# Depthwise-convolution taps all on VectorE at low scheduling priority, and the triangular inverse's masked copies as one VectorE operation

## The chip, the cores and the metric

One core of one Trainium2 chip. The metric is the device time of one execution of the whole program, in microseconds (us). Five engines run side by side, each through its own queue in order: TensorE (PE in the profile; its weight loads are PEld), VectorE (DVE), ScalarE (ACT), GpSimd (POOL) and SyncE (SP), which here issues the DMA transfers.

## The reference

Two blocks in a row over 512 tokens of width 1024. The first is a mixer with attention and a convolution branch, the second a linear-attention recurrence (RWKV-7 style) with a feed-forward part behind it. What matters here:

```python
def conformer_conv(glu_in, conv_w, conv_b, ln_w, ln_b, w_pw, b_pw):
    a, g = jnp.split(glu_in, 2, axis=-1)
    u = a * jax.nn.sigmoid(g)                       # 512 channels
    y = depthwise_conv(u, conv_w, width=31, centred) + conv_b
    y = jax.nn.silu(layer_norm(y, ln_w, ln_b))      # over channels
    return y @ w_pw + b_pw

# block 1
p = u @ w_in[l]                     # q, k, v, attention gate, GLU inputs, conv gate
attn = attend_blocked(q, k_all, v_all) * silu(p[..., ZA])
conv = conformer_conv(p[..., GLU], ...) * silu(p[..., ZC])
h = h + gate * (concatenate([attn, conv], -1) @ w_out[l])

# block 2, for every head, over 512 steps
def step(S, inp):
    r_t, w_t, k_t, v_t, a_t, b_t = inp
    sa = einsum('bhvk,bhk->bhv', S, a_t)
    S = S * w_t + outer(sa, b_t) + outer(v_t, k_t)
    return S, einsum('bhvk,bhk->bhv', S, r_t)
# then the feed-forward part: x + relu(rms_norm(x) @ w_ff1)**2 @ w_ff2
```

## The kernel before

Activations lie with features on the 128 partitions and the 512 tokens along the free side, so a tile is 128x512. Every fp32 projection is made of three reduced-precision matmuls: `split` (L140) makes a high part of a weight or an activation on ScalarE and the low part (what is left over) by a subtraction on VectorE, and `mm3` (L181) multiplies high by high, high by low and low by high. `Weights` (L160) streams 512 KB weight tiles in the order of use: DMA into `wr`, high part `wh` on ScalarE, low part `wl` on VectorE, with two `wr`, three `wh` and two `wl` buffers. One such weight tile feeds 24 matmuls of 512 columns. So `wl<-wr,wh` on VectorE stands ahead of every projection.

A scheduler orders the instructions of each engine when the program is built, by dependencies, by priorities (which follow the order of the code) and by its own picture of how long things take. From then on each engine works through its list in order and waits at whichever entry isn't ready.

Block 1 (`block1`, L345) runs in these stages:

- the modulation vectors and the first projections, up to about 84 us. They give three of the four GLU tiles (`glu`, L467; 128 channels each); the fourth comes of the projection pair `pa`, `pg`.
- then the q projection (four weight tiles), the context's norm (`modw` tiles) and the k/v projection (two weight tiles), eight gate projections (`zgate`, L595), the rotary embedding (`rope_q`, `rope_k`), a Newton iteration for the norms' square roots on VectorE (`newton`, L230, tiles `nr`), and the key tiles `kst`.
- attention: four head pairs by two halves. `scores` (L755) makes a 128x768 score tile `s` on TensorE, its maximum by a VectorE TENSOR_REDUCE, and the exponential on ScalarE; `values` (L775) transposes the result on TensorE, copies it on ScalarE (`xb`) and multiplies by the values into `pv`. There are 32 score tiles, and two buffers `s`.
- `ln_pw` (L697), a generator that the attention loop steps at the points of `LN_AFTER`: the LayerNorm over the convolution's result (a matmul with ones for the mean, four subtractions, four squares, a matmul for the variance, a square root, a broadcast by transposes, then scale, tanh and product), and the pointwise projection.
- the output projection (`xa` tiles), from about 344 us.

The convolution has 31 taps for each of four tiles `ys[i]` (tile name `hg`). The centre tap makes the tile; each of the other 30 adds a shifted copy of the input times one weight per channel. Before, these 120 are shared out by hand. `conv_pool` (L487) has ScalarE make the product (`cv`) and GpSimd add it, for tiles 0 and 1, 60 taps; `tick` paces it by the TensorE matmuls. `conv_self` (L511) does both on GpSimd, for 15 taps of tile 3. `conv_vec` (L521) does a tap as one VectorE scalar_tensor_tensor in place, 45 taps. The tables PACE, CVZ, CVQ, CONV and CSELF say how many go where.

Block 2 (`block2`, L1292) has six head pairs `p` by two halves `gi`, thus 12 passes of `gen_abc` (L945). A pass builds a unit lower-triangular system out of 64-token chunks and inverts it by block doubling in fp16: the 8x8 diagonal blocks first (`Dm`, `DT`, `P1`, `D2`, ...), then three levels of merging, where a level uses `OT[j]`, the system masked to the blocks of that level. `Lh` is the fp16 system and `k.m16` holds four fp16 masks. All these are 128x512 fp16 tiles named `f`. At the end, `IX` is identity minus the inverse, for one correction step. `OT` (three products a pass) and `IX` (one) run on GpSimd. So do the small Newton iterations of `prep` and `finish` (tiles `nr`, 128x8), which stay there. Projections for the next pairs fill TensorE in between. From 817 us on comes the feed-forward part.

Of the kernel before, what the change touches and what calls it, by code (L numbers as in the profile page):

```python
# [22 lines left out]
P = 128  # L23
# [136 lines left out]
class Weights:  # L160
# [172 lines left out]

LN_AFTER = (4, 4.5, 5, 5.5, 6.5, 7, 7.5, 7.5, 7.5, 8)
MODW = 10
PACE = 6
CVZ = (2, 1, 2, 0, 3, 4, 3, 3)
CVQ = (8, 9, 9, 8)
CTX = (0, 2)
CONV = (0, 0, 0, 0, 0, 0, 0, 0)  # L340
CSELF = (30, 0, 0, 1, 0, 1, 0, 0)
WARM = (8, 20, 0)
ZG = (1, 0, 1, 1, 1, 0, 0, 0, 0, 0, 0)

def block1(k, I, st, h1d):  # L345
# [130 lines left out]
    todo = [[w for w in range(31) if w != 15] for _ in range(4)]

    def tap(i):
        w = todo[i].pop(0)
        o0, o1 = max(0, 15 - w), min(S, S + 15 - w)  # L480
        return o0, o1, up[i][:, o0 + w - 15:o1 + w - 15], k.cw[:, i * 31 + w:i * 31 + w + 1]

    def conv_init(i):
        y = ys[i] = k.t("hg")
        A.activation(y, up[i], AF.Identity, scale=k.cw[:, i * 31 + 15:i * 31 + 16], bias=k.vec("conv_b", i))

    def conv_pool():  # L487
        r = yield
        for i in (0, 1):
            conv_init(i)  # L490
            while todo[i]:
                o0, o1, u, w = tap(i)
                p = k.t("cv")
                t = A.activation(p[:, o0:o1], u, AF.Copy, scale=w)
                if r is not None:
                    k.after(t, r)
                G.tensor_tensor(out=ys[i][:, o0:o1], in0=ys[i][:, o0:o1], in1=p[:, o0:o1], op=ALU.add)
                r = yield
        while True:
            yield  # L500

    cp = conv_pool()
    pace = [0]

    def tick(r, n=1):
        pace[0] += n
        while pace[0] >= PACE:
            pace[0] -= PACE
            cp.send(r)

    def conv_self(i, n):  # L511
        if ys[i] is None:
            y = ys[i] = k.t("hg")
            G.tensor_scalar(out=y, in0=up[i], scalar1=k.cw[:, i * 31 + 15:i * 31 + 16], scalar2=k.vec("conv_b", i), op0=ALU.mult, op1=ALU.add)
        for _ in range(min(n, len(todo[i]))):
            o0, o1, u, w = tap(i)
            p = k.t("cv")
            G.tensor_scalar(out=p[:, o0:o1], in0=u, scalar1=w, scalar2=None, op0=ALU.mult)
            G.tensor_tensor(out=ys[i][:, o0:o1], in0=ys[i][:, o0:o1], in1=p[:, o0:o1], op=ALU.add)

    def conv_vec(i, n):  # L521
        if ys[i] is None:
            conv_init(i)
        for _ in range(min(n, len(todo[i]))):
            o0, o1, u, w = tap(i)
            V.scalar_tensor_tensor(out=ys[i][:, o0:o1], in0=u, scalar=w, in1=ys[i][:, o0:o1], op0=ALU.mult, op1=ALU.add)

    def conv_drain():
        while todo[0] or todo[1]:
            cp.send(None)  # L530
        conv_vec(3, 31)
        assert not any(todo)

    W1 = Weights(k, [I["w_in"][0], I["w_in"][1]] + [I["w_q"][g] for g in range(4)] + [I["w_kv"][g] for g in range(2)]
                 + [I["w_in"][i] for i in (6, 7, 8, 9, 2, 3, 4, 5)] + [I["w_pw"][i] for i in range(2)] + [I["w_out"][i] for i in range(8)])
# [4 lines left out]
        mod_gate(g, mods[g])  # L540
    setup1(k, I)
    k.rest()
    next(cp)
    pa, pg = k.t("pj"), k.t("pv")
    proj(k, pa, W1.next(), us, tick=tick)
    proj(k, pg, W1.next(), us, tick=tick)
    glu(pa, pg)

    q_ps = [k.t("s", [2, S]), k.t("s", [2, S])]
    for g in range(4):  # L550
        wh, wl = W1.next()
        for kk in range(2):
            j = 2 * g + kk
            c = slice(kk * S, (kk + 1) * S)
            for t in range(4):
                tt = slice(t * P, (t + 1) * P)
                uh, ul = us[j]
                ps = q_ps[t // 2][:, t % 2, :]
                T.matmul(ps, uh[:, tt], wh[:, c], start=j == 0, stop=False)
                T.matmul(ps, uh[:, tt], wl[:, c], start=False, stop=False)  # L560
                tick(T.matmul(ps, ul[:, tt], wh[:, c], start=False, stop=j == KT - 1), 3)
        conv_vec(2, CVQ[g])
        if g == CTX[0]:
# [14 lines left out]
    for t in (2, 3, 4, 5, 0, 1):  # L578
        ps = k.t("pt", [256])
        for j in range(KT):  # L580
            wh, wl = kw[j // 4]
            c = slice((j % 4) * 256, (j % 4 + 1) * 256)
            uh, ul = cus[j] if t < 2 else us[j]
            o = (t if t < 2 else t - 2) * P
            tt = slice(o, o + P)
            T.matmul(ps, uh[:, tt], wh[:, c], start=j == 0, stop=False)
            T.matmul(ps, uh[:, tt], wl[:, c], start=False, stop=False)
            tick(T.matmul(ps, ul[:, tt], wh[:, c], start=False, stop=j == KT - 1), 1.5)
        kv = k.t("kvs", [256])
        A.activation(kv, ps, AF.Copy)  # L590
        kvs[t] = kv
# [2 lines left out]
    k.open(st, "zy", dict(kst=2))  # L594
    def zgate(tag):  # L595
        ps = k.t(tag)
        proj(k, ps, W1.next(), us, tick=tick)
        t = k.t("tA")
        A.activation(t, ps, AF.Tanh, scale=0.5)
        g = k.t("hg")  # L600
        V.scalar_tensor_tensor(out=g, in0=t, scalar=1.0, in1=ps, op0=ALU.add, op1=ALU.mult)
        return g
# [58 lines left out]
    def zgates(n):  # L661
        for _ in range(min(n, 8 - len(gz))):
            i = len(gz)
            gz.append(zgate(zt[i] if i < 4 else "pj"))
            conv_vec(3, CVZ[i])

    for i in range(4):
        rope_q(i)
# [139 lines left out]
    for pr in range(4):  # L808
        for half in range(2):
            i = 2 * pr + half  # L810
            pts = scores(pr, half, qs)
            zgates(ZG[3 + i])
            if i == int(LN_AFTER[0]):
                conv_drain()
            for _ in range(LN_AFTER.count(i)):
                next(ln, None)
            conv_vec(3, CONV[i])
            conv_self(3, CSELF[i])
            if half == 1 and pr < 3:
                qs = heads(pr + 1)  # L820
            if len(gz) == 8:
                while done:
                    att_split(done.pop(0))
            if pend is not None:
                if pend[1] == 0:
                    pv = k.t("pv")
                values(*pend, pv)
                if pend[1] == 1:
                    att_out(pend[0], pv)
                    done.append(pend[0])  # L830
            for _ in range(LN_AFTER.count(i + 0.5)):
                next(ln, None)
            pend = (pr, half, pts)
# [111 lines left out]
def gen_abc(k, p, pd, gi):  # L945
# [72 lines left out]
    units(ps, Dm, DT, True, True)  # L1018
    D2T = ev(ps)
    yield  # L1020
    OT = []
    for j in range(1, 4):
        o = k.t("f", [4, P], F16)
        G.tensor_tensor(out=o, in0=Lh, in1=mk(j), op=ALU.mult)
        OT.append(o)
    ps = k.t("i")
    units(ps, D2, D2T, True, True)
    D4T = ev(ps)
# [16 lines left out]
    tok(1)  # L1045
    for j in range(3):
        ps = k.t("i")
        units(ps, OT[j], X, True, True)
        Y = k.t("f", [4, P], F16)
        V.tensor_tensor(out=flat(Y), in0=ps, in1=flat(k.id16x4), op=ALU.add)  # L1050
        yield
        ps = k.t("i")
        units(ps, XT, Y, True, True)
        ps2 = k.t("i")
        units(ps2, Y, XT, True, True)
        X, XT = ev(ps), ev(ps2)
        if j == 0:
            b = k.t("i")
            for u in range(4):
                mm(b[:, u * 64:(u + 1) * 64], MT[:, u, :], Vs[:, u % 2, (u // 2) * 64:(u // 2) * 64 + 64], start=True, stop=True)  # L1060
            A.activation(R4[:, :, 64:128], b[:, 0:256].rearrange("p (u d) -> p u d", u=4), AF.Copy)
        yield
    ps = k.t("i")
    IX = k.t("f", [4, P], F16)
    G.tensor_tensor(out=IX, in0=k.id16x4, in1=X, op=ALU.subtract)
    for u in range(4):
        mm(ps[:, u * P:(u + 1) * P], Lh[:, u, :], X[:, u, :], start=True, stop=False)
        mm(ps[:, u * P:(u + 1) * P], Ll[:, u, :], X[:, u, :], start=False, stop=True)
# [223 lines left out]
def block2(k, I, nm, h1d, out):  # L1292
    A, V, T, G, Y = k.A, k.V, k.T, k.G, k.Y
    P2 = ExitStack()
    k.open(P2, "p2b", dict(lw=1, wa=1, r1=1, AR=2, BK=2, vs=2, UX=2, MT=1, E=3, R4=2, Vs=2, UV=3, W=2, QG=2, sb=2, st=2, f=18))
    k.open(P2, "p2s", dict(s=1), PSUM)
    k.open(P2, "p2i", dict(i=3), PSUM)
    k.open(P2, "p2y", dict(y=1), PSUM)
# [325 lines left out]
```

## Time and profile before

| | us |
|---|---|
| median of 3 runs (1193.18 to 1193.87) | 1193.24 |
| the profiled execution | 1195.04 |
| its span, first to last instruction | 1193.2 |
| PE busy in the span | 1096.6 (92%) |
| DVE busy | 750.1 (63%) |
| ACT busy | 573.7 (48%) |
| POOL busy | 266.3 (22%) |

The profiled execution lies 1.84 us over its own span and the median 0.04 us over that span, so that a change of the span can be taken off the median as it is. The shares are averages over stages of different kinds: PE is busy throughout the last third and far from it between 98 and 226 us, while DVE is the reverse.

### The profile page before, as it was taken

The numbers are of one execution on the slowest core, as the hardware profiler recorded it, in microseconds if no ns is written. First come the engines' busy times: TensorE is split into PE (matmuls) and PEld (weight loads), VectorE is DVE, ScalarE is ACT, GpSimd is POOL, SyncE is SP. The second block draws the span as 40 slices with busy tenths as digits, with TensorE's granted clock in tenths as the row PEclk, the third lists the DMA queues.
The fourth block names the chain that finished last, engine by engine and source line by source line (L and its number), as shares of the span: only waits on it lengthen the run. The fifth ranks groups of instructions, "written<-read, shape, count | busy, mean of one in ns | idle before, by whom it ended". The sixth has DMA issues, their size and how long they took to land.

```text
span 1193.2 us, 16090 instructions
## 1 busy us (share of the span) xinstructions
PE 1096.6 (92%) x6268; PEld 842.1 (71%) x6268; DVE 750.1 (63%) x1161; ACT 573.7 (48%) x1047; POOL 266.3 (22%) x360
## 2 busy tenths in 40 slices
PE   7997776799999888999999988999999999999998
PEld 3665664565677766666667766776888888888887
DVE  3348999756545469888887688856544334334332
ACT  4346456567843436545464566556534224223220
POOL 0018558780000223334242234100000000000000
PEclk7999887899999989999999999999999999999999
DMA  8752111100123411101011211221232323232332
GB/s 289 251 199 71 36 46 61 53 19 7 48 84 137 123 52 36 37 19 37 19 36 37 62 50 62 72 71 54 88 106 89 105 90 104 90 102 93 99 113 88
DMA packets 30604, 96.47 MB, mean 81 GB/s; under 512 B 3392, under 2 KB 4160, under 8 KB 30528
## 3 DMA queue, kind: packets, MB, share of 16 engines
q1 hardware_dynamic: 30528, 95.45, 24.4%
q8 instruction: 49, 0.80, 0.3%
q14 instruction: 27, 0.22, 0.1%
HBM read 91.24 MB, written 4.19 MB: 80 GB/s over the span
## 4 chain that ended last, share of the span: by engine, by line
PE 72%; DVE 17%; ACT 5%; POOL 3%; issue 2%; DMA 1%; SPq 0%; DVEq 0%; ACTq 0%; POOLq 0%
PE pf L57 29%; PE pj L57 19%; PE i L57 6%; PE pt L57 6%; PE s L57 5%; DVE f L57 5%; PE pv L57 4%; DVE hg L57 3%; PE y L57 2%; POOL nr L57 2%; DVE wl L57 2%; DVE tA L57 1%; DVE p L57 1%; ACT p L57 1%; DVE nr L57 1%
## 5 line engine op out<-in xcount | busy, mean ns | idle before, releaser
L57 ACT ACTIVATE wh<-wr 128x1024 fp32r<-128x1024 f32 (+1 forms) x132 | 137.4, 1042 | 155.0 <-PE pf L57 76.4
L57 DVE TENSOR_TENSOR wl<-wr,wh 128x1024 fp32r<-128x1024 f32 (+1 forms) x132 | 162.3, 1230 | 20.6 <-PE pt L57 7.6
L57 PE MATMUL pj<-hg,wh 128*128 128x512 f32 x448 | 156.3, 417 | 3.2 <-ACT r L57 1.8
L57 PE MATMUL pf<-A,wh 128*128 128x512 f32 x512 | 157.8, 389 | 0.0
L57 POOL TENSOR_TENSOR hg<-hg,cv 128x497 f32<-128x497 f32 (+14 forms) x75 | 112.7, 1503 | 124.3 <-ACT cv L57 116.7
L57 ACT ACTIVATE f<-i 128x512 f16<-128x512 f32 (+1 forms) x132 | 73.2, 598 | 105.1 <-PE i L57 104.9
L57 PEld LDWEIGHTS pf<-A,wh 128*128 128x128 f32 x512 | 95.9, 188 | 19.9
L57 PE MATMUL pf<-A,wl 128*128 128x512 f32 x256 | 99.6, 389 | 0.0
L57 PEld LDWEIGHTS pj<-hg,wh 128*128 128x128 f32 x448 | 81.5, 192 | 19.9 <-ACT r L57 2.0
L57 DVE TENSOR_TENSOR x<-x,pf 128x512 f32<-128x512 f32 (+1 forms) x33 | 22.1, 671 | 113.9 <-PE pf L57 113.9
L57 PE MATMUL i<-f 128*128 128x128 f16 x816 | 69.7, 224 | 24.0 <-DVE f L57 23.6
L57 PE MATMUL pj<-hg,wl 128*128 128x512 f32 x224 | 90.0, 402 | 1.5 <-DVE wl L57 1.5
L57 PEld LDWEIGHTS <-f 128*128 128x128 f16 x864 | 56.7, 100 | 48.5 <-DVE f L57 24.9
L57 PE MATMUL pf<-ff,wh 128*128 128x512 f32 (+1 forms) x272 | 79.7, 377 | 0.0
L57 PE MATMUL pf<-hg,wh 128*128 128x512 f32 x256 | 78.8, 389 | 0.0
L57 DVE SCALAR_TENSOR_TENSOR fr<-pf,r 128x512 f32<-128x512 f32 x32 | 22.1, 691 | 85.4 <-PE pf L57 82.1
L57 ACT ACTIVATE fr<-fr 128x512 f32<-128x512 f32 x32 | 20.2, 632 | 100.2 <-DVE fr L57 100.2
L57 POOL TENSOR_TENSOR f<-f,c 128x512 f16<-128x512 f16 x36 | 48.0, 1361 | 74.1 <-ACT f L57 74.1
L57 PE MATMUL pj<-U,wh 128*128 128x512 f32 x160 | 53.6, 408 | 10.7 <-DVE hg L57 10.7
L57 POOL TENSOR_SCALAR nr<-nr 128x8 f32<-128x8 f32 (+2 forms) x70 | 24.9, 355 | 171.2 <-DVE nr L57 129.1
L57 PEld LDWEIGHTS pf<-ff,wh 128*128 128x128 f32 x272 | 50.1, 188 | 9.5
L57 PEld LDWEIGHTS pf<-hg,wh 128*128 128x128 f32 x256 | 48.0, 188 | 10.0
(303 smaller groups left out, 2368.0 us busy)
## 6 DMA issues: line engine op xcount, KB each, us to landing
wr<-w_ff SPq DMA_DIRECT2D x64, 512.0 KB, 3.5
modw<-w_mod SPq DMA_DIRECT2D x24, 512.0 KB, 7.2
wr<-rw_in SPq DMA_DIRECT2D x20, 512.0 KB, 3.5
wr<-w_out SPq DMA_DIRECT2D x16, 512.0 KB, 3.5
wr<-w_in SPq DMA_DIRECT2D x10, 512.0 KB, 3.5
wr<-w_start SPq DMA_DIRECT2D x8, 384.0 KB, 3.7
x<-xT SPq DMA_DIRECT2D x8, 256.0 KB, 5.7
wr<-w_q SPq DMA_DIRECT2D x4, 512.0 KB, 3.7
```

What stands on the lines that cost most here:

```text
L57: r = f(*a, **kw)
```

## The change

All 120 taps become VectorE scalar_tensor_tensor instructions. `conv(i)` emits the centre tap on ScalarE and the 30 others under a lowered scheduling priority: tiles 0 to 2 ahead of the projections `pa` and `pg`, tile 3 behind them. The generator, its pacing, the tables and the `cv` buffers go. In `gen_abc`, the three products `OT` become one VectorE product of 128x1536 elements into a new tile `lv` (two buffers; the pool `f` goes from 18 to 12), with `Lh` broadcast over the three masks, and `IX` moves to VectorE.

```diff
+LATER = 1500
-PACE = 6 ... CSELF = (30, 0, 0, 1, 0, 1, 0, 0)
...
-    def conv_pool(): ...   def tick(r, n=1): ...   def conv_self(i, n): ...
-    def conv_vec(i, n): ...   def conv_drain(): ...
+    def conv(i):
+        u, cw = up[i], lambda w: k.cw[:, i * 31 + w:i * 31 + w + 1]
+        y = ys[i] = k.t("hg")
+        A.activation(y, u, AF.Identity, scale=cw(15), bias=k.vec("conv_b", i))
+        with k.tc.high_priority(offset=-LATER):
+            for w in range(31):
+                if w != 15:
+                    o0, o1 = max(0, 15 - w), min(S, S + 15 - w)
+                    V.scalar_tensor_tensor(out=y[:, o0:o1], in0=u[:, o0 + w - 15:o1 + w - 15], scalar=cw(w), in1=y[:, o0:o1],
+                                           op0=ALU.mult, op1=ALU.add)
...
-    next(cp)
+    for i in range(3):
+        conv(i)
     pa, pg = k.t("pj"), k.t("pv")
-    proj(k, pa, W1.next(), us, tick=tick)
-    proj(k, pg, W1.next(), us, tick=tick)
+    proj(k, pa, W1.next(), us)
+    proj(k, pg, W1.next(), us)
     glu(pa, pg)
+    conv(3)
...
-    OT = []
-    for j in range(1, 4):
-        o = k.t("f", [4, P], F16)
-        G.tensor_tensor(out=o, in0=Lh, in1=mk(j), op=ALU.mult)
-        OT.append(o)
+    OT = k.t("lv", [3, 4, P], F16)
+    V.tensor_tensor(out=OT, in0=Lh.rearrange("p (o u) x -> p o u x", o=1).to_broadcast([P, 3, 4, P]),
+                    in1=k.m16[:, 1:4].rearrange("p (j o) x -> p j o x", o=1).to_broadcast([P, 3, 4, P]), op=ALU.mult)
...
-        units(ps, OT[j], X, True, True)
+        units(ps, OT[:, j], X, True, True)
...
-    G.tensor_tensor(out=IX, in0=k.id16x4, in1=X, op=ALU.subtract)
+    V.tensor_tensor(out=IX, in0=k.id16x4, in1=X, op=ALU.subtract)
```

The order of the instructions moves at three places that matter.

VectorE in the q projection; `wl` is the low part of the next weight tile, `hg<-hg,c_83` a tap, `tA<-tA` the context norm's sum. Before, and then in the changed program:

```order
L57 TENSOR_TENSOR wl<-wr,wh 128x1024 x2
L57 SCALAR_TENSOR_TENSOR hg<-tA,pj 128x512
L57 SCALAR_TENSOR_TENSOR hg<-hg,c_83 128x497
L57 SCALAR_TENSOR_TENSOR hg<-hg,c_83 128x498
L57 SCALAR_TENSOR_TENSOR hg<-hg,c_83 128x499
L57 TENSOR_TENSOR wl<-wr,wh 128x1024
L57 SCALAR_TENSOR_TENSOR hg<-hg,c_83 128x500
L57 TENSOR_TENSOR tA<-tA 128x256
```

```order
L57 TENSOR_TENSOR wl<-wr,wh 128x1024
L57 SCALAR_TENSOR_TENSOR hg<-hg,c_83 128x500
L57 SCALAR_TENSOR_TENSOR hg<-hg,c_83 128x499 x2
L57 SCALAR_TENSOR_TENSOR hg<-hg,c_83 128x501
L57 SCALAR_TENSOR_TENSOR hg<-hg,c_83 128x500 x2
L57 SCALAR_TENSOR_TENSOR hg<-hg,c_83 128x502
L57 TENSOR_TENSOR wl<-wr,wh 128x1024
L57 SCALAR_TENSOR_TENSOR hg<-tA,pj 128x512
L57 TENSOR_TENSOR tA<-tA 128x256
```

The taps of three tiles now run in turn between two low parts of weights, 5 to 7 of them, from the second weight tile on. Ahead of the first score maximum stand 62 taps on VectorE where 45 stood, and the other 58 stand among the 32 maxima, the last one ahead of the last maximum.

TensorE where LayerNorm begins (`pj<-hg,c_83` is the mean, `pj<-g,tA` the variance, `pj<-g,c_83` the broadcast, `s<-kst,xa` scores, `pt<-g,p` transposes and `pv<-xb,kvs` products of `values`, `pt<-g,tA` a broadcast of `att_out`, `pj<-U` the pointwise projection). Before, after 20 of 32 scores:

```order
L57 MATMUL pj<-hg,c_83 128x512 x4
L57 MATMUL pv<-xb,kvs 64x256 x4
L57 MATMUL pt<-g,p 128x128 x8
L57 MATMUL s<-kst,xa 128x512
L57 MATMUL pv<-xb,kvs 64x256 x4
```

In the changed program, three of the four mean matmuls stand there, and the rest behind the last score:

```order
L57 MATMUL s<-kst,xa 128x256 x2
L57 MATMUL pj<-hg,c_83 128x512
L57 MATMUL pj<-g,tA 128x1 x4
L57 MATMUL pj<-g,c_83 128x128 x4
L57 MATMUL pt<-g,tA 128x128 x4
L57 MATMUL pj<-U,wh 128x512 x2
L57 MATMUL pj<-U,wl 128x512
```

The LayerNorm's remaining steps follow each other with no attention work between them in TensorE's list; 12 of the 48 `values` chunks (four transposes each) and most of the pointwise projection stand behind them.

VectorE in a pass of the inverse (`f<-UX` is `Dm`, `f<-f,c` are `DT` and `P1`, `lv` the three masked copies, `BK` and `p` belong to the next pair's preparation). Before, and then in the changed program:

```order
L57 TENSOR_TENSOR f<-UX,c_3149 128x512
L57 TENSOR_TENSOR f<-f,c_3149 128x512 x2
L57 TENSOR_TENSOR f<-i,c_3149 128x512
L57 SCALAR_TENSOR_TENSOR p<-p 128x512
L57 TENSOR_TENSOR sb<-y,g 128x128
L57 TENSOR_SCALAR p<-p 128x512
L57 TENSOR_SCALAR p<-p,c_3149 128x512
L57 TENSOR_TENSOR BK<-p 128x4x2x64
```

```order
L57 TENSOR_TENSOR f<-UX,c_2999 128x512
L57 TENSOR_TENSOR f<-f,c_2999 128x512 x2
L57 TENSOR_TENSOR f<-i,c_2999 128x512
L57 SCALAR_TENSOR_TENSOR p<-p 128x512
L57 TENSOR_TENSOR lv<-f,c_2999 128x1536
L57 TENSOR_SCALAR p<-p 128x512
L57 TENSOR_SCALAR p<-p,c_2999 128x512
L57 TENSOR_TENSOR BK<-p 128x4x2x64
```

The masked copies stand behind the four operations that the next matmuls need; `IX` (not shown) stands one or two places behind them, ahead of the correction step's addition.

## Rows read from the trace of the kernel before

**Rows 1.** Stretches: length, then busy us of PE, PEld, DVE, ACT, POOL, clock, DMA.
```profile
84.00:98.00 14.00, 14.00 (x63) 11.52 (x63) 8.59 (x13) 8.99 (x14) 11.40 (x9) 1.00 0.18 45
98.00:226.00 128.00, 90.13 (x406) 74.29 (x405) 122.80 (x166) 73.72 (x133) 86.11 (x57) 0.83 0.17 53
226.00:320.00 94.00, 86.27 (x530) 58.94 (x529) 59.96 (x103) 71.47 (x132) 37.45 (x26) 1.00 0.07 23
...
435.00:785.00 350.00, 321.10 (x2609) 243.09 (x2608) 292.50 (x522) 193.46 (x446) 114.53 (x216) 0.98 0.13 43
...
817.00:1193.00 376.00, 371.89 (x1668) 308.90 (x1668) 158.84 (x192) 119.82 (x151) 0.00 (x0) 1.00 0.30 96
```

**Rows 2.** DVE in time, 102 to 114 us: start, duration, operation, shapes, count.
```profile
102.57 2.30 DVE L57 TENSOR_TENSOR wl<-wr,wh 128x1024 fp32r<-128x1024 f32 x1
...
106.80 0.73 DVE L57 SCALAR_TENSOR_TENSOR hg<-hg,c 128x501 f32<-128x501 f32 x1
107.46 0.41 DVE L57 TENSOR_TENSOR tA<-tA 128x256 f32<-128x256 f32 x1
...
111.90 1.75 DVE L57 SCALAR_TENSOR_TENSOR hg<-hg,c 128x504 f32<-128x504 f32 x1
113.56 1.21 DVE L57 TENSOR_TENSOR wl<-wr,wh 128x1024 fp32r<-128x1024 f32 x1
```

**Rows 3.** POOL in time, the same stretch.
```profile
103.86 2.15 POOL L57 TENSOR_TENSOR hg<-hg,cv 128x509 f32<-128x509 f32 x1
108.09 5.01 POOL L57 TENSOR_TENSOR hg<-hg,cv 128x510 f32<-128x510 f32 x3 [2.08 <-ACT cv L57]
```

**Rows 4.** DVE's groups, 97 to 217 us: busy us, mean ns, idle before.
```profile
L57 DVE SCALAR_TENSOR_TENSOR hg<-hg,c 128x497 f32<-128x497 f32 (+14 forms) x45 | 50.3, 1118 | 1.3 <-ACT hg L57 1.1
L57 DVE TENSOR_TENSOR wl<-wr,wh 128x1024 fp32r<-128x1024 f32 x11 | 17.0, 1546 | 1.1 <-PE pt L57 1.1
...
L57 DVE TENSOR_TENSOR tA<-tA 128x256 f32<-128x256 f32 x7 | 6.1, 871 | 0.0
...
L57 DVE TENSOR_TENSOR modw<-tA,modw 128x256 fp32r<-128x256 f32 x8 | 5.2, 674 | 0.0
L57 DVE TENSOR_TENSOR q<-xb 128x256 f32<-128x256 f32 x8 | 5.0, 660 | 0.0
```

**Rows 5.** PE in time, context norm: the idle time before it in brackets.
```profile
121.93 1.01 PE L57 MATMUL pj<-g,tA 128*128 128x1 f32 x4 [10.68 <-DVE tA L57]
```

**Rows 6.** Chain that ended last, in time: start, duration, what.
```profile
89.49 5.45 PE pv L57 x24
...
292.34 1.28 ACT L57
...
509.83 4.00 DVE f L57 x4
...
849.27 340.35 PE pf L57 x1524
```

**Rows 7.** POOL's groups, whole span.
```profile
L57 POOL TENSOR_TENSOR hg<-hg,cv 128x497 f32<-128x497 f32 (+14 forms) x75 | 112.7, 1503 | 124.3 <-ACT cv L57 116.7 <-DVE c L57 3.9
...
L57 POOL TENSOR_TENSOR f<-c,f 128x512 f16<-128x512 f16 x12 | 15.5, 1289 | 39.4 <-ACT f L57 33.2 <-DVE p L57 6.1
```

**Rows 8.** DVE's groups, 226 to 320 us.
```profile
L57 DVE TENSOR_REDUCE c<-s 128x1 f32<-128x768 f32 x31 | 29.4, 955 | 21.6 <-PE s L57 21.6
...
L57 DVE TENSOR_TENSOR hg<-hg,pj 128x512 f32<-128x512 f32 x8 | 5.0, 682 | 2.3 <-PE pj L57 2.3
```

**Rows 9.** ACT in time, LayerNorm inside the attention loop.
```profile
284.04 0.63 ACT L57 ACTIVATE tA<-hg 128x512 f32<-128x512 f32 x1 [1.83 <-DVE hg L57]
```

**Rows 10.** DVE's groups, 435 to 785 us.
```profile
L57 DVE TENSOR_TENSOR f<-f,c 128x512 f16<-128x512 f16 x24 | 29.2, 1254 | 0.0
...
L57 DVE TENSOR_TENSOR BK<-p 128x512 f32<-128x512 f32 x10 | 11.0, 1103 | 0.0
```

**Rows 11.** DVE in time, the last pass of the inverse.
```profile
739.85 0.68 DVE L57 TENSOR_TENSOR f<-UX,c 128x512 f16<-128x512 f32 x1
740.45 0.76 DVE L57 TENSOR_TENSOR f<-f,c 128x512 f16<-128x512 f16 x2
```

**Rows 12.** Who waited for whom, whole span: us in total, times, longest.
```profile
PE i L57 <- DVE f L57: 23.6, 28, 6.4
```

More of the change, by code (lines that the diff above doesn't have):

```diff
@@ L335 @@
 MODW = 10
-PACE = 6
-CVZ = (2, 1, 2, 0, 3, 4, 3, 3)
-CVQ = (8, 9, 9, 8)
+LATER = 1500
 CTX = (0, 2)
-CONV = (0, 0, 0, 0, 0, 0, 0, 0)
-CSELF = (30, 0, 0, 1, 0, 1, 0, 0)
 WARM = (8, 20, 0)
@@ L474, in block1 @@
     ys = [None] * 4
[L476 to L483, printed above, removed]
-        y = ys[i] = k.t("hg")
[L485 to L532, printed above, removed]
+    def conv(i):
+        u, cw = up[i], lambda w: k.cw[:, i * 31 + w:i * 31 + w + 1]
+        y = ys[i] = k.t("hg")
+        A.activation(y, u, AF.Identity, scale=cw(15), bias=k.vec("conv_b", i))
[5 more added lines that the diff above has]
+                                           op0=ALU.mult, op1=ALU.add)
@@ L560, in block1 @@
                 T.matmul(ps, uh[:, tt], wl[:, c], start=False, stop=False)
-                tick(T.matmul(ps, ul[:, tt], wh[:, c], start=False, stop=j == KT - 1), 3)
-        conv_vec(2, CVQ[g])
+                T.matmul(ps, ul[:, tt], wh[:, c], start=False, stop=j == KT - 1)
         if g == CTX[0]:
@@ L587, in block1 @@
             T.matmul(ps, uh[:, tt], wl[:, c], start=False, stop=False)
-            tick(T.matmul(ps, ul[:, tt], wh[:, c], start=False, stop=j == KT - 1), 1.5)
+            T.matmul(ps, ul[:, tt], wh[:, c], start=False, stop=j == KT - 1)
         kv = k.t("kvs", [256])
@@ L596, in zgate @@
         ps = k.t(tag)
-        proj(k, ps, W1.next(), us, tick=tick)
+        proj(k, ps, W1.next(), us)
         t = k.t("tA")
@@ L664, in zgates @@
             gz.append(zgate(zt[i] if i < 4 else "pj"))
-            conv_vec(3, CVZ[i])
     for i in range(4):
@@ L812, in block1 @@
             zgates(ZG[3 + i])
-            if i == int(LN_AFTER[0]):
-                conv_drain()
             for _ in range(LN_AFTER.count(i)):
                 next(ln, None)
-            conv_vec(3, CONV[i])
-            conv_self(3, CSELF[i])
             if half == 1 and pr < 3:
@@ L1294, in block2 @@
     P2 = ExitStack()
-    k.open(P2, "p2b", dict(lw=1, wa=1, r1=1, AR=2, BK=2, vs=2, UX=2, MT=1, E=3, R4=2, Vs=2, UV=3, W=2, QG=2, sb=2, st=2, f=18))
+    k.open(P2, "p2b", dict(lw=1, wa=1, r1=1, AR=2, BK=2, vs=2, UX=2, MT=1, E=3, R4=2, Vs=2, UV=3, W=2, QG=2, sb=2, st=2, f=12, lv=2))
     k.open(P2, "p2s", dict(s=1), PSUM)
@@ L1506, in emit @@
         p1 = ExitStack()
-        k.open(p1, "p1", dict(c1=1, U=16, tA=4, kvs=6, cv=2))
+        k.open(p1, "p1", dict(c1=1, U=16, tA=4, kvs=6))
         k.open(p1, "p1m", dict(pj=1), PSUM)
```

## The prediction

> **What bounds the kernel now.** I read the stretches first [rows 1]. From 817 us on TensorE is busy 371.9 of 376 us: that third can't move, and the change touches nothing in it. From 98 to 226 us VectorE is busy 122.8 of 128 us and TensorE only 90.1, at a mean granted clock of 0.83 (a mixture of the two levels, since TensorE rests in between); one wait of TensorE there is 10.68 us for a small VectorE sum [rows 5]. So VectorE bounds this stretch. From 226 to 320 us TensorE is busy 86.3 of 94 and VectorE 60. From 435 to 785 us TensorE has 321 of 350 and VectorE 292.5.
>
> Next I asked why VectorE is full, by single instructions in time beside GpSimd's. At 106.8 us a tap takes 0.73 us (its successor starts 0.66 us later) and a 256-wide sum 0.41, while GpSimd rests (it ended at 106.0). At 111.9, in the middle of three GpSimd additions, the same tap takes 1.75 us; a `wl` takes 2.30 at 102.6 and 1.21 at 113.6 [rows 2, 3]. So VectorE's instructions come in two sizes here, and the long ones lie where GpSimd has an operation under way. Part of VectorE's load is waiting on GpSimd.
>
> **The change part by part.**
>
> *Time to the first score maximum (226 us).* The excess over the free sizes, by groups [rows 4], with the free sizes of [rows 2]: 45 taps x (1.118 - 0.73) = 17.5 us; 11 `wl` x (1.55 - 1.21) = 3.7; 7 sums x (0.87 - 0.41) = 3.2; the two other 256-wide groups, 16 x (0.67 - 0.41) = 4.1; together 28.5. The smaller groups of that view taken in the same way hold about 13 more (an estimate: their free sizes are those of the same shapes at moments when GpSimd rests), and 84 to 98 us about 4. Sum 46. VectorE's busy time from 84 to 226 us is 8.6 + 122.8 = 131.4 [rows 1]; without the excess 85. The order puts 62 taps ahead of the first maximum where 45 stood: 17 x 0.65 = 11 more, so 96.5 us of work. Starting at 84 us that ends at 180.5 us. TensorE's own sum is near that: 24 matmuls of one weight tile take 5.45 us [rows 6]; 13 such tiles and a k/v projection worth three make 16 x 5.45 = 87 us, with small matmuls 91, thus 175 us. Two engines so nearly equal, each in its own order, lose something to each other: I add 4 us and take 184.5, a gain of **42 us**. Bounds: 36 (10 us lost) to 46 (none). The clock should come back by itself if TensorE no longer rests, and the 5.45 is already its price at full clock.
>
> ScalarE loses 60 products and GpSimd 75 additions and 15 products (the additions stand in [rows 7]); neither engine was the limit. The emptier ScalarE delivers `wh` sooner, which costs nothing and earns nothing as long as `wl` comes later.
>
> *Attention up to the last maximum.* 58 taps x 0.65 = 38 us are added to VectorE; the LayerNorm's arithmetic of some 12.6 us (8 subtractions and products are 5.0 of it [rows 8]) goes behind the last maximum, and GpSimd's hindrance of some 3 us goes. 60 + 38 - 12.6 - 3 = 82 of 94 us. VectorE waited 21.6 us for scores here [rows 8], so most taps fit in waits; but a tap that has begun delays a maximum by up to 0.65 us. TensorE has two `s` buffers to cover one such delay. I take 93 us, as long as before: what LayerNorm no longer interrupts (a 1.28 us table load in the chain at 292 us [rows 6], and its matmuls of about 5 us) pays for the taps. Bounds: 8 us less, 8 us more.
>
> *LayerNorm behind the last score.* Before, attention work lay between its steps. Now TensorE's list holds nothing to do between mean, variance, broadcast and the first pointwise matmul. The chain, of VectorE steps of 0.62 to 0.68 [rows 8] and ScalarE steps of 0.63 [rows 9]: four subtractions 2.5, square 0.6, addition 0.7, variance 0.5, root and reciprocal 0.5, broadcast 0.65, product 0.65, two activations 1.4, product 0.7, high part 0.6 = 9 us, with up to two table loads of 1.28. About 9 us of it is idle TensorE, and some 5 us of matmuls moved here from the loop. It gives back **14 us**; bounds 8 and 18.
>
> *The inverse.* The free fp16 product is 0.76 us for two [rows 11]; the mean of the 24 is 1.254 against 0.42 for one, so 24 x 0.83 = 20 us are hindrance by the GpSimd copies next to them; `BK` has 10 x (1.10 - 0.68) = 4 [rows 10]. Added: 12 times a 1536-element copy and `IX`. No row shows the former. Its ends are 0.42 (one 512-element copy) and 1.26 (three); an fp16 512 takes as long as an fp32 256 (0.41), so by the fp32 slope (512 takes 0.68) 1536 should cost 0.68 + 0.28 = 0.96, say 0.9 in sequence: nearer to three. `IX` 0.35. 12 x 1.25 = 15 us. VectorE wins 9 us on balance; but order matters more than sum. The chain holds a group of four `f` of 4.00 us [rows 6]; without hindrance it is 0.6 + 0.35 + 0.35 + 0.6 = 1.9, and the masked copies stand behind it. `IX` goes from 1.29 on GpSimd [rows 7] to 0.35. TensorE's waits for these `f` sum to 23.6 us, 28 times [rows 12]. I take two thirds of that, **15 us**, since a shortened wait lets TensorE run into the next one. Bounds: 4 and 27 (all of it and a little of the projections).
>
> Sum: 1193.2 - 42 + 0 + 14 - 15 = 1150, rounded down by 1 for the clock: **1149 us**. The profiled execution's span and the median are equal within 0.1 us, so nothing is added.
>
> **A rule that speaks against it.** VectorE is busy 96% of the stretch to 226 us [rows 1], and the change hands it 75 more taps. The Trainium skill, "Perfetto Trace Analysis", section "Optimizing Scalar/DVE Operations", says that where DVE is saturated some work may well be offloaded to Scalar or even GPSIMD, the opposite of this change. The same passage warns that GPSIMD and DVE share a read port, so that moving work between those two might not help; rows 2 and 3 side with the warning.
>
> **The rivals.**
> 1. *The long sizes stay* (VectorE simply full; nothing of the 46 us comes back). For it: 96% busy. Against: the short and long sizes of one shape, and where they lie [rows 2, 3]. Price: 17 taps x 1.12 = 19 us to the first maximum, 14 for LayerNorm, nothing won in the inverse: 1226 us. It is what the rule's first half would give. Chance 0.02.
> 2. *Taps delay every score.* VectorE takes a maximum only when it has done the taps ahead of it, and TensorE waits for a free `s`. For it: VectorE's sum of 82 of 94 us, and runs of up to seven taps in the order. Against: the 21.6 us of waiting, and that nearly every maximum has only one tap ahead. Won elsewhere: 42 + 15 - 14 = 43 us, so it decides from 43 / 32 = 1.35 us (two taps) a score. With three taps a score, 32 x 1.96 = 63 us: 1212 us, slower. Chance 0.05.
> 3. *Attention and LayerNorm give back more*: 8 us among the taps and 18 behind, the inverse only 6, the first stage 40: 1193 - 40 + 8 + 18 - 6 = 1173. Chance 0.18.
> 4. *Both engines run free*: 46 won, attention 6 shorter, LayerNorm 9, the inverse 22: 1128. Chance 0.10.
> 5. *All of it returns* in later waits, within 0.2% (2.4 us, about what a measurement of this kernel can tell from no change). Chance 0.02.
>
> **How the numbers follow.** The forecast has 0.63 (its own range 1136 to 1162). Rivals 3 and 4 lie on its side: faster 0.91; same 0.02; slower 0.07 (rivals 1, 2). From 1130 to 1174 the range takes in the forecast, rival 3 and half of rival 4 and leaves out under 0.2.
>
> **What would show it.** Right: taps of 0.73 us throughout and `wl` of 1.21; the first score maximum near 184 us; TensorE's clock near 1.0 from 98 us on; the last maximum near 278; a TensorE gap of about 9 us behind it; `f<-f,c` of 0.42 with `lv` near 0.95; TensorE's waits for `f` under 10 us. Wrong: taps still over 1 us (rival 1), maxima that TensorE's scores wait for (rival 2), a `lv` of 1.7 us, or another VectorE row, such as `z` or `BK`, that takes the place of `f` in the chain.

## The result, and the profile after

The changed kernel takes 1150.57 us (median of 4 runs, 1149.1 to 1154.9) against 1193.21 us before: a ratio of 0.9654, 95% interval 0.9622 to 0.9685. The forecast was 1149 us, in a range of 1130 to 1174. The profiled execution has a span of 1147.3 us, 45.9 less than that of before.

The stretches of the changed kernel; columns as in [rows 1]. They run from the eleventh weight tile's `wl` to the first score maximum, from there to the last maximum, and from there to the first weight tile of block 2; the fourth is the recurrence, between two of its matmuls.

```profile
84.20:172.00 87.80, 83.28 (x446) 70.72 (x445) 87.02 (x180) 43.70 (x84) 0.00 (x0) 1.00 0.27 84
172.00:260.60 88.60, 81.09 (x492) 54.27 (x490) 80.47 (x140) 58.25 (x110) 0.00 (x0) 1.00 0.08 25
260.60:349.10 88.50, 77.29 (x359) 57.77 (x359) 46.04 (x67) 43.70 (x66) 0.00 (x0) 0.90 0.24 81
402.30:725.90 323.60, 306.60 (x2503) 231.84 (x2502) 262.39 (x524) 184.44 (x427) 50.79 (x168) 0.97 0.14 45
```

The same four stretches of the kernel before, cut at the same points of the program to within 0.4 us:

```profile
90.00:226.50 136.50, 98.63 (x444) 81.34 (x443) 125.57 (x170) 79.78 (x142) 93.18 (x61) 0.84 0.18 54
226.50:320.40 93.90, 86.17 (x528) 58.62 (x527) 60.28 (x104) 71.62 (x132) 36.95 (x26) 1.00 0.07 23
320.40:386.50 66.10, 65.87 (x323) 50.24 (x324) 32.66 (x45) 28.77 (x44) 0.00 (x0) 1.00 0.32 108
438.00:771.50 333.50, 304.60 (x2503) 229.69 (x2502) 279.61 (x500) 183.71 (x428) 114.00 (x216) 0.98 0.14 43
```

In the first row the stretch to the first score maximum is 49 us shorter, VectorE does more instructions (180 for 170) in 38.5 us less, GpSimd does nothing, and TensorE's mean granted clock is 1.00 where it was 0.84. The second row (the 32 maxima) is 5 us shorter, although VectorE has 20 us more to do. The third (from the last maximum to block 2) is 22 us longer. The fourth, the recurrence, is 10 us shorter.

| point of the program | before, us | after, us | moved by, us | of it in this step |
|---|---|---|---|---|
| ninth weight tile's `wl` begins | 75.2 | 71.5 | -3.7 | -3.7 |
| first score maximum | 226.5 | 172.0 | -54.5 | -50.8 |
| last score maximum | 320.4 | 260.6 | -59.8 | -5.2 |
| first weight tile of block 2 | 386.5 | 349.2 | -37.3 | +22.4 |
| FFN begins | 839.6 | 794.0 | -45.6 | -8.3 |
| end | 1193.2 | 1147.3 | -45.9 | -0.3 |

VectorE's groups of the changed kernel, 84 to 172 us (busy us, mean ns, idle before), which answer to [rows 4]:

```profile
L57 DVE TENSOR_TENSOR wl<-wr,wh 128x1024 fp32r<-128x1024 f32 x14 | 16.9, 1216 | 0.8 <-issue 0.6
L57 DVE SCALAR_TENSOR_TENSOR hg<-hg,c 128x509 f32<-128x509 f32 x6 | 4.4, 741 | 0.0
...
L57 DVE TENSOR_TENSOR tA<-tA 128x256 f32<-128x256 f32 x7 | 2.9, 412 | 0.0
```

Every group has its short size: 1.22, 0.74 and 0.41 us, where [rows 4] had 1.55, 1.12 and 0.87.

TensorE of the changed kernel in time around the last maximum (start, duration, the idle time before in brackets):

```profile
259.64 0.96 PE L57 MATMUL s<-kst,xa 128*128 128x512 f32 x4 [1.26 <-ACT p L57]
260.68 1.13 PE L57 MATMUL pj<-hg,c 128*128 128x512 f32 x2
266.58 1.86 PE L57 MATMUL pj<-g,tA 128*128 128x1 f32 x8 [4.77 <-DVE tA L57]
269.01 1.11 PE L57 MATMUL pj<-g,c 128*128 128x128 f32 x4 [0.57 <-DVE c L57]
275.74 1.11 PE L57 MATMUL pt<-g,tA 128*128 128x128 f32 x4 [5.62 <-ACT tA L57]
```

Three gaps, 4.77, 0.57 and 5.62 us, stand between mean, variance, broadcast and the next work: 11 us in all, and TensorE's mean granted clock is 0.90 over the stretch. In the recurrence two groups of VectorE's answer to [rows 10], and one wait to [rows 12]:

```profile
L57 DVE TENSOR_TENSOR lv<-f,c 128x1536 f16<-128x1536 f16 x12 | 11.4, 949 | 0.0
...
L57 DVE TENSOR_TENSOR f<-f,c 128x512 f16<-128x512 f16 x24 | 9.0, 418 | 0.0
```

```profile
PE i L57 <- DVE f L57: 5.3, 6, 2.9
PE y L57 <- ACT x L57: 4.8, 4, 2.4
```

### The profile page after: what moved, and what is told of

Read it like the earlier page. It is cut to its first block, busy times and chain, and to the rows that moved or that the text cites. A ratio compares the mean times of both kernels' runs of the same rounds, so it can differ in the third digit from the quotient of the medians.

```text
span 1147.3 us, 15927 instructions
## 1 busy us (share of the span) xinstructions
PE 1084.9 (95%) x6268; PEld 835.6 (73%) x6268; DVE 728.2 (63%) x1260; ACT 538.3 (47%) x987; POOL 66.9 (6%) x222
## 4 chain that ended last, share of the span: by engine, by line
PE 81%; DVE 7%; ACT 4%; POOL 3%; issue 2%; DMA 2%; SPq 0%; ACTq 0%; DVEq 0%; POOLq 0%
PE pf L57 30%; PE pj L57 23%; PE i L57 7%; PE s L57 7%; PE pt L57 6%; PE pv L57 4%; PE y L57 3%; POOL nr L57 3%; DVE hg L57 2%; ACT p L57 1%; DVE c L57 1%; DVE wl L57 1%; DVE tA L57 1%; ACT wh L57 1%; DMA wr<-w_in 1%
## 5 line engine op out<-in xcount | busy, mean ns | idle before, releaser
L57 DVE TENSOR_TENSOR wl<-wr,wh 128x1024 fp32r<-128x1024 f32 (+1 forms) x132 | 158.6, 1203 | 11.8 <-ACT wh L57 4.5
L57 DVE SCALAR_TENSOR_TENSOR hg<-hg,c 128x498 f32<-128x498 f32 (+14 forms) x120 | 84.8, 735 | 0.4
L57 PEld LDWEIGHTS <-f 128*128 128x128 f16 x720 | 46.0, 100 | 23.6 <-issue 14.3
L57 PE MATMUL i<-f 128*128 128x128 f16 x672 | 55.7, 224 | 5.7 <-DVE f L57 5.3
L57 PEld LDWEIGHTS pf<-A,wl 128*128 128x128 f32 x256 | 48.0, 188 | 10.1
L57 PE MATMUL pf<-ff,wl 128*128 128x512 f32 (+1 forms) x136 | 51.2, 376 | 0.0
```

Source lines behind the costliest of these rows:

```text
L57: r = f(*a, **kw)
```

## The experiments

Theory: VectorE's operations on two SBUF tensors become long while GpSimd has an operation under way; the change ends that. The convolution's part gives it back in the first stretch, pays some of it for the other taps and the LayerNorm, and the inverse's part gives 10 us of its own. Rivals: the gain lies in the work that GpSimd and ScalarE no longer hand on, or in VectorE's new order. "Excess" is the duration of an instruction less that of the same instruction in the changed kernel, summed over VectorE's instructions that lie beside a long GpSimd operation.

**The two parts apart.** `conv_only` is the changed kernel with the inverse's part undone (the diff below); `inv_only` is the kernel before with these lines changed the other way.

```diff
-    OT = k.t("lv", [3, 4, P], F16)
-    V.tensor_tensor(out=OT, in0=Lh.rearrange("p (o u) x -> p o u x", o=1).to_broadcast([P, 3, 4, P]),
...
+    for j in range(1, 4):
+        o = k.t("f", [4, P], F16)
+        G.tensor_tensor(out=o, in0=Lh, in1=mk(j), op=ALU.mult)
...
-    V.tensor_tensor(out=IX, in0=k.id16x4, in1=X, op=ALU.subtract)
+    G.tensor_tensor(out=IX, in0=k.id16x4, in1=X, op=ALU.subtract)
...
```

> Only the convolution's part of the change: 120 taps on VectorE, while the masked copies and IX of the inverse stay on GpSimd. Theory (the two parts are independent, the convolution gives what the traces show to the start of block 2): the traces put the start of block 2 37 us earlier, of which up to 4 us may be chance at the very start, and the recurrence 10 us shorter; so this kernel takes 1193.2 - 35 = about 1158 to 1161 us, with passes of the inverse again 53 to 54 us apart per head pair. Rival (the parts add differently: the inverse's gain comes from the convolution's leftovers, such as the pools' places): about 1150 us, with passes 52 us apart.

> Only the inverse's part: masked copies and IX on VectorE, the convolution as before. Theory: 10 us less than before, about 1183 us; TensorE's waits for f fall from 23.6 to about 5 us and f<-f,c from 1.25 to 0.42 us. Rival (the inverse gains nothing alone): 1193 us within 2.

`conv_only` takes 1163.14 us, 0.9751 (0.9724 to 0.9778) of the kernel before; `inv_only` 1184.1 us, 0.9915 (0.9887 to 0.9943). On the same chip the kernel before took 1193.77. So the parts give 30.6 and 9.7 us, each known to about 3 us, together 40.3 of the 42.6 of both, and the theory holds: the parts are independent as far as this can tell. In `conv_only` TensorE waits 23.6 us for `f`, as before, and in `inv_only` 5.3, as after. `conv_only` is 2 us above its expectation; its first stretch took 91.2 us for the same VectorE work of 87.0, with TensorE's mean granted clock at 0.96 instead of 1.00.

**GpSimd work that nobody needs.** Three kernels add 68 GpSimd operations to the changed kernel, one of these lines each (`dummy_two`, `dummy_one`, `dummy_set`), at every sixth matmul of the projections. VectorE's list stays the same to the row.

```diff
+    d0, d1, dmo = k.t("cv"), k.t("cv"), k.t("cv")
...
+    k.after(G.tensor_tensor(out=dmo[:, 0:504], in0=d0[:, 0:504], in1=d1[:, 0:504], op=ALU.add), r)
+    k.after(G.tensor_scalar(out=dmo[:, 0:504], in0=d0[:, 0:504], scalar1=0.5, scalar2=None, op0=ALU.mult), r)
+    k.after(G.memset(dmo[:, 0:504], 0.0), r)
...
```

> The changed kernel with 68 additional additions on GpSimd, two operands of 128x504 fp32 in the SBUF, which nobody reads, paced by the projections' matmuls as the additions before were; VectorE's order is the same to the row. Theory (VectorE's instructions become long while GpSimd has an operation under way): taps rise from 0.73 to about 1.1 us and wl from 1.21 to about 1.55 in the projections; 86 us of GpSimd in 98 to 226 us went with 45 us of excess before, so 68 x 1.5 = 102 us bring back 35 to 50 us: the first score maximum at about 210 us and 1185 to 1198 us in all. Rival (the gain came from the work that GpSimd and ScalarE no longer hand on, or from VectorE's new order): taps stay at 0.73, 1150 us within 3.

> The same with 68 GpSimd products of one SBUF operand of 128x504 fp32 and a constant, in place of the additions. Theory a (any GpSimd operation that reads the SBUF holds VectorE up): the loss per us of GpSimd time is that of the additions, about 0.45 us. Theory b (only operations with two tensors do): 1150 us within 3, taps at 0.73. The trace of before can't decide: its GpSimd products and additions lay side by side.

> As the additional GpSimd additions and products, but 68 settings of 128x504 to zero, which read nothing. If what GpSimd reads stretches VectorE's instructions (68 additions gave 38 us of excess, 68 products of one operand 10), this gives none: taps at 0.73 us, 1150 us within 3. If GpSimd's writing does it too, 3 to 10 us of excess and 1153 to 1160 us.

Their pacing did not work: `k.after` orders the program's lists and makes no wait on another engine, so all 68 ran back to back from the start, the additions until 112 us. The place was missed, the question was still answered: 1175.31 us with additions, 1161.13 with products, which lies between its two theories, 1150.26 with settings. Over 102.5 us of additions VectorE had 39 us of excess, over 109.7 us of products 11, over 35.3 us of settings none. Of the 39 us, 27.5 lay ahead of the ninth weight tile's `wl`, where VectorE has waits, and moved it by only 17; the end moved by 25. VectorE of `dummy_two` in time, with an addition of GpSimd always under way (`qc` and `kc` have the same shape):

```profile
100.01 1.34 DVE L57 TENSOR_TENSOR qc<-rt,c 128x128 f32<-128x128 f32 x1
101.28 0.28 DVE L57 TENSOR_TENSOR kc<-rt,c 128x128 f32<-128x128 f32 x1
101.48 1.34 DVE L57 TENSOR_TENSOR qc<-rt,c 128x128 f32<-128x128 f32 x1
102.75 0.28 DVE L57 TENSOR_TENSOR kc<-rt,c 128x128 f32<-128x128 f32 x1
```

```profile
L57 POOL TENSOR_TENSOR cv<-cv 128x504 f32<-128x504 f32 x68 | 102.5, 1508 | 5.3
```

A `qc` of 0.28 us takes 1.34, then a `kc` its 0.28; the pair repeats every 1.47 us, close to GpSimd's 1.51 for one addition. VectorE gets in once per addition, then waits for the next to end. That the small operation loses as much as a tap says that it waits, and isn't slowed. Beside GpSimd products of one tensor the same kind of instruction grows by at most 0.42 us, though a product takes as long (1.61 us).

**The same, with real pacing.** `paced` gives ScalarE 60 products and GpSimd 60 additions that wait for them, as before the change; VectorE keeps its 120 taps, 65 of them ahead of the first maximum, so that its order is not the same to the row.

```diff
...
+                k.after(A.activation(p[:, 0:504], up[pace[1] % 2][:, 0:504], AF.Copy, scale=0.5), r)
+                G.tensor_tensor(out=dmo[:, 0:504], in0=dmo[:, 0:504], in1=p[:, 0:504], op=ALU.add)
...
```

> The changed kernel, its 120 taps on VectorE, with 60 products on ScalarE and 60 additions on GpSimd besides, of 128x504, which nobody reads, each addition waiting for its product and each product placed by the projections' matmuls as before the change; 65 taps stand ahead of the first maximum. It loads the two engines as the kernel before did, without taking anything from VectorE. Theory (the additions stretch VectorE's instructions by about 0.37 us for each us of GpSimd time, as the unpaced additions did: 38 us for 102): 60 x 1.5 x 0.37 to 0.5 = 33 to 45 us more VectorE time in the projections, where VectorE has no waits: the first maximum at 205 to 218 us, 1180 to 1193 us in all. Rival (the stretched instructions fit into waits, and the change's gain lay elsewhere): under 1165 us.

1202.92 us, 1.0064 (1.0043 to 1.0086) of the kernel before: the whole gain is gone, and more. The first maximum comes at 236.0 us, 160.9 us after the ninth `wl` for 100.5 in the changed kernel; of these 60 us more, 54 are excess beside 94.3 us of additions, 2 are three more taps, and 5 are waits. VectorE and GpSimd of `paced` in time:

```profile
96.11 2.26 DVE L57 TENSOR_TENSOR wl<-wr,wh 128x1024 fp32r<-128x1024 f32 x1
98.29 4.63 DVE L57 SCALAR_TENSOR_TENSOR hg<-hg,c 128x500 f32<-128x500 f32 x7
102.85 1.22 DVE L57 TENSOR_TENSOR wl<-wr,wh 128x1024 fp32r<-128x1024 f32 x1
103.98 0.68 DVE L57 SCALAR_TENSOR_TENSOR hg<-tA,pj 128x512 f32<-128x512 f32 x1
104.58 5.17 DVE L57 SCALAR_TENSOR_TENSOR hg<-hg,c 128x501 f32<-128x501 f32 x4
```

```profile
95.73 1.56 POOL L57 TENSOR_TENSOR cu<-cu,cv 128x504 f32<-128x504 f32 x1
103.73 1.47 POOL L57 TENSOR_TENSOR cu<-cu,cv 128x504 f32<-128x504 f32 x1 [6.44 <-ACT cv L57]
106.17 3.04 POOL L57 TENSOR_TENSOR cu<-cu,cv 128x504 f32<-128x504 f32 x2 [0.97 <-ACT cv L57]
```

The `wl` at 96.11 lies beside an addition: 2.26 us. Then GpSimd rests from 97.3 to 103.7, and seven taps take 4.63 us, 0.66 each. The operation at 103.98 lies beside an addition wholly, but reads `pj` from PSUM: 0.68, its usual time. The four taps behind it take 5.17. This settles theory against rivals: additions and products that nobody needs were put back, no tap was taken from VectorE, and the time went back. The expectation's top was 1193, since it took 0.5 us of excess per us of additions; it was 54/94.3 = 0.57, and TensorE's mean granted clock was 0.82 besides, near the 0.84 before the change.

**The inverse in the same way.** `inv_dummy` adds six GpSimd products to each pass where the masked copies stood; VectorE's list is again the same.

```diff
+    for j in range(1, 4):
+        for h in (0, 2):
+            fd = k.t("fd", [2, P], F16)
+            G.tensor_tensor(out=fd, in0=Lh[:, h:h + 2], in1=mk(j)[:, 0:2], op=ALU.mult)
...
```

> The changed kernel with six products on GpSimd in each of the twelve passes of the inverse, of two SBUF tensors of 128x256 fp16, which nobody reads, at the place where the masked copies of the kernel before stood and with the same input; VectorE's order is the same to the row. It tells whether the inverse's gain of 10 us is the end of the stretching (theory a: f<-f,c goes from 0.42 back to 1.0 to 1.25 us, TensorE's waits for f from 5 back to 15 to 24 us, 6 to 10 us more in all: about 1158 us) or the later arrival of results that GpSimd computed (theory b: nothing waits for these products, so 1150 us within 2).

1168.96 us, 18 more than the changed kernel. VectorE's group and TensorE's wait in `inv_dummy`:

```profile
L57 DVE TENSOR_TENSOR f<-f,c 128x512 f16<-128x512 f16 x24 | 19.4, 847 | 0.0
```

```profile
PE i L57 <- DVE f L57: 19.2, 22, 5.7
```

The wait for `f` goes from 5.3 back to 19.2 us, with nobody waiting for the products themselves: theory a. It costs more than the whole part had given, and more than the 1158 us expected. The fourth stretch is 15.9 us longer than in the changed kernel; 13.9 of them are this wait. TensorE's other idle time stays at the 12 us of the changed kernel, where it was 5 in the kernel before: so the wait comes back and those other waits stay. Hindrance isn't greater than before the change: VectorE's excess in this stretch is 21 us, against 30 in the kernel before, though the masked copies are stretched too (their mean goes from 0.95 to 1.18 us).

**Where the other taps and the LayerNorm go.** Only LATER, how far behind in priority the taps stand, is changed.

```diff
-LATER = 1500
+LATER = 800
```

`later1000` and `later300` have 1000 and 300 there.

> The changed kernel with LATER = 800 in place of 1500: the order up to the first maximum stays as it is (62 taps ahead of it), but the other 58 taps now stand ahead of the 22nd of the 32 maxima, and the LayerNorm's steps between the 22nd and the last, with scores between them in TensorE's list. Theory (the 22 us that the stretch from the last maximum to the first weight tile of block 2 grew by, 66 to 88.5 us, are the LayerNorm's chain left without cover): that stretch falls to 70 to 76 us, attention grows by up to 5, and the time is 1133 to 1143 us. Rival (the chain only moves, and maxima wait for it and for denser taps): 1148 to 1153 us.

> The changed kernel with LATER = 1000: between 800 and 1500, all taps done by the 28th maximum, the LayerNorm's first subtractions behind the 28th, the second behind the last. Theory (the 58 taps and the LayerNorm cost some 13 to 17 us between the first maximum and block 2 wherever they stand; 160 us before, 177 with 1500, 173 with 800): 172 to 178 us for that stretch, 1145 to 1151 us in all. Rival (there is a good place between): that stretch under 168 us, under 1141 us.

> The changed kernel with LATER = 300: all 120 taps ahead of the first maximum, attention and LayerNorm in the order of the kernel before. Theory (VectorE bounds the stretch to the first maximum, and the taps among the maxima cost next to nothing): 58 more taps x 0.65 = 38 us there, so the first maximum at about 210 us instead of 172; attention 86 to 89 us; from the last maximum to block 2 66 us again, 22 less; 1150 + 38 - 2 - 22 = 1160 to 1168 us. Rival (TensorE bounds that stretch and VectorE has room): the first maximum before 185 us, under 1140 us.

`later800` takes 1146.09 us, `later1000` 1148.79, `later300` 1178.82. The stretches between first maximum, last maximum and block 2, of `later800` and then of `later300` (whose first row is the stretch to the first maximum):

```profile
172.20:278.90 106.70, 91.09 (x528) 62.12 (x526) 92.31 (x162) 72.69 (x132) 0.00 (x0) 0.95 0.07 21
278.90:345.20 66.30, 66.07 (x324) 50.36 (x324) 32.57 (x45) 28.78 (x44) 0.00 (x0) 1.00 0.32 108
```

```profile
83.70:218.40 134.70, 90.24 (x442) 75.00 (x441) 124.81 (x242) 43.35 (x84) 0.00 (x0) 0.81 0.16 51
218.40:313.70 95.30, 88.96 (x533) 60.57 (x532) 58.37 (x105) 72.35 (x133) 0.00 (x0) 0.98 0.09 28
313.70:379.80 66.10, 65.87 (x323) 50.27 (x324) 32.55 (x45) 28.78 (x44) 0.00 (x0) 1.00 0.33 108
```

In `later800` the stretch behind the last maximum is back at 66.3 us, better than expected, but the maxima take 106.7 instead of 88.6, where up to 5 more were expected. TensorE's wait for a free `s` (it is put down to ScalarE's exponential, which reads it) grows there from 3.7 to 10.9 us. Of 22 us of uncovered chain only 4 were to be had: the rival's mechanism, with a small gain. From the first maximum to block 2 it is 160 us before, 177 after, 173 in `later800`, 175 in `later1000`, 161 in `later300`. So 58 taps cost 13 to 17 us there in each of the three orders that have them. Put ahead of the first maximum, the same taps cost 46 us (172 to 218.4), more than the 38 expected, since VectorE also waits 10 us, and TensorE's mean granted clock is 0.81; with the maxima at 95.3 us, not 86 to 89, this more than covers the 11 us by which `later300` lies above the top of its expectation. `later800` has the lowest median of all: 0.9592 (0.9565 to 0.9619) of the kernel before; from `later1000`, 0.9611 (0.9579 to 0.9642), it can't be told apart.

**One step beyond.** `l8_nr` moves the small Newton steps of the recurrence from GpSimd to VectorE, with LATER = 800; the other three calls are changed in the same way.

```diff
-    newton(k, k.G, rn, kss[:, 0:8], floor=1e-24)
+    newton(k, k.V, rn, kss[:, 0:8], floor=1e-24)
```

> LATER = 800 and, beyond the change, the Newton steps of the recurrence's four normalisations (10 small operations in a row, 13 times) on VectorE instead of GpSimd, so that GpSimd has nothing left in the recurrence. By the trace a group takes some 5 us from its first to its last GpSimd operation, and about seven groups lie in the chain of waits. Theory (such a chain lies open there): on VectorE a group takes some 1.5 to 2 us, TensorE's idle time of 25 us between 349 and 726 us falls by a third: 6 to 10 us less than LATER = 800 alone. Rival (VectorE's 13 x 2 = 26 us more work delays f and p as much): within 2 us of LATER = 800 alone, or slower.

1149.24 us against 1146.09 for `later800`: no gain, the rival. The recurrence of `later800` and then of `l8_nr`, from the first matmul on `f` to the last:

```profile
398.50:722.10 323.60, 306.81 (x2493) 231.48 (x2493) 260.53 (x520) 184.22 (x427) 50.67 (x168) 0.96 0.14 45
```

```profile
402.20:722.00 319.80, 307.03 (x2489) 230.87 (x2489) 272.25 (x686) 184.21 (x427) 0.00 (x0) 0.97 0.14 43
```

It is 3.8 us shorter, all of it idle time of TensorE (12.8 for 16.8 us), where a third of 25 was expected; and the work behind it up to the FFN is 3.8 us longer (72.0 against 68.2). What comes there later was not followed further. Of the 3.7 us by which this profile's span is the longer, 3.5 stand ahead of the first maximum already, where the edit changes nothing: point 5 below has their cause.

## Why the prediction was right, step by step

The time was right (1149 said, 1150.6 measured) and so was the mechanism. That the sum came so near is luck in part: the terms missed by 9 and 5 us and by an unforeseen 4 on one side, and by 8 and 7 us on the other, and two of them lie outside their own bounds.

1. *First maximum, -42 us said, -50.8 measured*, outside its bounds of 36 and 46. The excess was 48.7 us, not 46 (the instructions of 84 to 226 us of the kernel before, by the sizes of the changed kernel), and all of it went: every group is at its free size. The order's 62 taps were there too. The step that failed is what was left of VectorE's waits. From the ninth `wl` to the first maximum it had waited 16 of 151 us, and now waits 3 of 100: 12.6 less. The sum counted from 84 us on only, where it took off the 10.6 us of waits and put 4 back for two engines that lose something to each other, 6.6 less. That loss was 0.8: 87.0 us of work in 87.8. And 7 of the taps ran before 84 us, among waits, where the sum had put all 17 additional ones behind. `later300`, with 10 us lost, shows that this loss is no constant.
2. *Attention, 0 said, -5.2 measured; LayerNorm, +14 said, +22.4 measured*, outside its bounds of 8 and 18. The step that failed is what the chain leaves to do behind the last maximum: the idle time was 11 us for the 9 said, but TensorE's busy time there rose by 11.4 us (65.9 to 77.3, with the matmuls moved there and the mean granted clock at 0.90), not by 5. Together they are +17 for +14. They are one term, as `later800` shows: where the LayerNorm returns into the loop, the loop grows by 18.
3. *The inverse, -15 said, -10 measured* (and -8.3 with the preparation of the first pair). `f<-f,c` at 0.42, `lv` at 0.95 and TensorE's wait under 10 us were as forecast. The step that failed is "two thirds of 23.6": 18.3 us of that wait went, but TensorE's idle time fell only from 28.9 to 17.0 us, since other waits grew by 6 (for ScalarE's `x` from 0.8 to 4.8 us, the largest). TensorE's busy time rose by 2 us, which is within what it varies by itself there (point 5).
4. *The clock* is 1.00 to the first maximum, as said. In `paced` and `later300`, where TensorE waits for VectorE there (busy 97.1 of 140 and 90.2 of 134.7 us), its mean is 0.82 and 0.81, between the two levels, as in the kernel before.
5. *Not foreseen*: 3.7 us at the start, before anything of the change runs. The experiments show it to be chance. The stretch from 20 to 30 us of `later1000` and then of `later800`, whose edits change nothing there:

```profile
20.00:30.00 10.00, 7.91 (x31) 4.04 (x25) 4.41 (x9) 5.94 (x8) 0.00 (x0) 0.66 0.66 229
```

```profile
20.00:30.00 10.00, 7.77 (x40) 5.13 (x35) 4.90 (x10) 5.95 (x8) 0.00 (x0) 1.00 0.65 227
```

The mean granted clock there is 0.66 to 0.67, a mixture of the two levels, in the profiles of the kernel before, `conv_only`, `l8_nr`, `paced` and `later1000`, and their ninth `wl` begins at 74.4 to 75.2 us; it is 0.98 to 1.00 in those of the changed kernel, `inv_only`, `dummy_one`, `dummy_set`, `inv_dummy`, `later800` and `later300`, where it begins at 71.0 to 73.2 (`dummy_two`, disturbed there, is left out). Kernels with the same start fall on both sides. So about 3 of the 45.9 us between the two profiles are no effect of the change, which fits the 42.6 between the medians. The recurrence has such a spread too: nine profiles with the same order of TensorE's and VectorE's instructions in block 2 (the changed kernel's, `inv_only`'s, the three `dummy` kernels', `paced`'s and the three `later` kernels') take 318.0 to 323.6 us from the first matmul on `f` to the last, with TensorE idle for 16.5 to 17.4 us in each and a mean granted clock of 0.98 in the shortest and 0.96 in the longest. The kernel before and `conv_only` take 329.4 and 329.6 us with 27 idle, so that the gain of the inverse is clear of it; a difference of 3 us between two medians is not.

Rival 1 (the long sizes stay) and rival 2 (taps delay every score so far that all is lost) are refuted by the sizes and by the 88.6 us of the maxima. Rival 3 gave the LayerNorm 18 us, nearer to the 22.4 than the forecast's 14; rival 4 had the first stretch (46) and attention (6 shorter) nearer than the forecast, and LayerNorm and inverse further off.

## What to carry to other kernels

Before work is shared out to GpSimd, compare one shape of VectorE's in time with and without a GpSimd operation beside it: where it has two sizes, VectorE's busy share holds waiting, and a full engine can be emptied by giving it more work. Price what the new work displaces as one term with what it delays, from stage to stage: a chain that is moved under cover takes the cover from something else. And compare the start of two profiles, where both programs are the same, before a few us at the end are explained.

## What was not expected of the hardware

How much VectorE loses depends on what GpSimd reads, not only on how long it is busy. With the same list on VectorE it lost 0.38 us per us of additions of two tensors back to back (39 / 102.5), 0.10 per us of products of one tensor (11 / 109.7, at most 0.42 us for an instruction), and nothing beside 35.3 us of settings: 29 of its instructions lay beside these, up to 43.5 us, and the additions cost 13 us over the same stretch. It depends on VectorE's load too: in `paced`, where VectorE was busy 152.6 of 160.9 us from the ninth `wl` to the first maximum, it lost 0.57 per us of additions. VectorE's operations with an operand in PSUM lose nothing (0.68 us beside an addition), nor do its reductions of an SBUF tensor (`c<-xb`, 128x512: 0.68 us in the changed kernel, 0.67 wholly beside an addition in `paced`). Its operations with scalars on a single SBUF tensor do lose: `tA<-tA,c`, a TENSOR_SCALAR of 128x256, takes 0.41 us in the changed kernel and 0.88 in the mean, 1.36 at most, in `paced`. So two tensors, as the theory above has it, are not needed on VectorE's side. The Trainium skill, "SBUF — State Buffer", section "SBUF: two separate sides", says that VectorE's operations with two SBUF inputs and GpSimd's operations that read the SBUF exclude each other for the whole instruction. The additions, the PSUM operand and the settings agree with it; the products don't, since VectorE's instructions beside them lose 0.42 us at most of the 1.61 that one takes, and here the measurement decides.
